# Gated DeltaNet in a hybrid encoder: the transposes of a scan's output stand behind the next head's local part

## The chip, the cores and the metric

The kernel runs on one core of one Trainium2 chip. The metric is the device time of one execution in microseconds (us); lower is better. The core's engines are TensorE (PE; its weight loads are listed apart as PEld), VectorE (DVE), ScalarE (ACT), GpSimd (POOL) and SyncE (SP), which issues the DMAs here. Each engine works through its own instructions in the order in which they stand in the program, and semaphores make one wait for another.

## The reference

An encoder of two layers over 512 tokens of width 1024, all in float32. Layer 0 mixes the tokens with a gated DeltaNet of 8 heads of width 128, layer 1 with HGRN2. Behind each mixer comes a squared-ReLU MLP (1024 to 4096 and back), and at the end an RMSNorm.

```python
for i in range(DEPTH):                      # DEPTH = 2
    y = _rmsnorm(h, norm_mix[i])
    if i % N_MIXERS == 0:
        y = _gated_deltanet(y, gdn_w_in[j], gdn_conv[j], ..., gdn_onorm[j], gdn_w_out[j])
    else:
        y = _hgrn2(y, hgrn_w_in[j], lower_bounds[i], hgrn_gnorm[j], hgrn_w_out[j])
    h = h + y
    h = h + _sq_relu_mlp(_rmsnorm(h, norm_mlp[i]), mlp_w_up[i], mlp_w_down[i])
return _rmsnorm(h, norm_final)
```

The gated DeltaNet projects the input to q, k, v and a gate, runs a short causal convolution and SiLU over q, k and v, normalises q and k, and then works through the tokens of each head in chunks. Per chunk a triangular system is solved, and a state S (128 x 128) is carried from chunk to chunk:

```python
def step(S, xs):
    qd, a_c, u_c, w_c, kd, dl = xs
    v_new = u_c - einsum('bhck,bhkv->bhcv', w_c, S)
    o = einsum('bhck,bhkv->bhcv', qd, S) + einsum('bhij,bhjv->bhiv', a_c, v_new)
    S = S * dl[..., None, None] + einsum('bhck,bhcv->bhkv', kd, v_new)
    return S, o
```

The output o of each head is normalised to unit mean square, scaled by a learned vector, multiplied with the gate and projected by `gdn_w_out`.

## The kernel before

**Numbers and tiles.** Every large product is made of three matmuls of reduced float32 (fp32r): both factors are split into a high and a low part, and lines 125 to 127 add high x high, high x low and low x high. One such matmul takes a 128 x 128 block of the weights and all 512 tokens (128x512 in the profile). `weights` loads a slice of the weights by a DMA of 1 MB on SP's queue (line 108, two buffers `raw`), ScalarE casts the high part (line 114), VectorE subtracts for the low part (line 115). A chunk is 128 tokens here, four per head (NC = 4).

**One head of the DeltaNet** goes through these functions:

- `gdn_conv`: the projections `pj` of q, k and v of the head, the convolution on VectorE and ScalarE (lines 389 to 393).
- `gdn_local`: what needs no state. TensorE transposes k (`pk`, line 436); ScalarE squares it with sums over rows (438), VectorE scales it (440). The same for q (`pq`, lines 443 and 445), then for v (`pv`, line 456, scaled by ScalarE in line 458). A matmul `pe` spreads the decay (462, used on VectorE in 465). Then `pga`, the products of k with k and q (475, in two halves), from which VectorE makes the triangular matrix `n` (477) and the attention matrix `aa` (479). The last line 479 is the last VectorE step of this function.
- `gdn_inverse`, for two heads at once: the triangular matrices are inverted from 32 x 32 blocks up. The first stages are many matmuls of 32x32 (`px`, line 513, and `pu`, line 520), copied out on ScalarE (516), with masks and transposes on VectorE (506 to 508, 522, 523); later stages are lines 531 to 558.
- `gdn_scan`: four chunks one after the other. Per chunk `pks` (585) and VectorE's remainder `r` (587), `pw` with the inverse (590) and VectorE's `wv` (592), the update of the state `ps` (595) and VectorE's `s` (598 or 600), the output `po` (602 and 604). Behind the last chunk: ScalarE squares the output with row sums (611), VectorE adds up `xo` (612 to 614), the inverse root takes two steps on ScalarE and three on VectorE (`rsqrt`, lines 149 to 153), ScalarE scales the output by it (617, into a buffer that the trace names `wlo`), TensorE transposes the four chunks (`pt`, line 620), VectorE multiplies with the learned vector and writes `oh` (622).
- `gdn_gated`: `oh` times the gate, split for the output projection.

**Order.** `gdn` (lines 271 to 323) interleaves the heads: round j projects head j + 1, runs the scan of an earlier head, the local part of head j, and in every second round the inverse of heads j - 2 and j - 1. The scans of heads 0 to 4 come in rounds 3 to 7, which have a local part; those of heads 5, 6 and 7 come in rounds 8 and 9, which have none.

```python
GATES = ((), (), (), (), (0,), (), (1,), (), (2,), (3,))
SCANS = ((), (), (), (0,), (1,), (2,), (3,), (4,), (5,), (6, 7))
```

A scheduler sets each engine's order from the program order, from the dependences, and from priorities: what stands under `high_priority` comes ahead of projections as soon as its inputs are there by the scheduler's reckoning, and projections fill the rest. `after(i, prev)` adds a dependence of the kind NoSync: it orders instruction i behind prev for the scheduler, and sets no semaphore between engines.

**PSUM.** The products of scan and local part share the tag "ma" with two banks (`mix`); head 7's scan and the inverse use "mb" with three; projections have three banks of their own (`acc`). A new tile takes the bank of the oldest and waits until that one's readers are done.

Of the kernel before, what the change touches and what calls it, by code (L numbers as in the profile page):

```python
# [15 lines left out]
ALU = mybir.AluOpType  # L16
PSUM = bass.MemoryType.PSUM

T, D, HID, NH, P = 512, 1024, 4096, 8, 128
# [3 lines left out]
NC = T // P  # L23
# [7 lines left out]
SCANS = ((), (), (), (0,), (1,), (2,), (3,), (4,), (5,), (6, 7))  # L31


class Net:
# [236 lines left out]
    def gdn(self, first):  # L271
        nc, a = self.nc, self.a
        self.emask = self.const("emask", [P, P])
        self.conv = self.const("conv", [P, 3 * NH, 4])
        self.onorm = self.const("onorm", [P, 1])
        self.pick = self.const("pick", [4 * NH, 2 * NH])
        alog = self.cp.tile([P, NH], F32, tag="alog", name="alog")
        nc.sync.dma_start(out=alog, in_=a["alog"].partition_broadcast(P))
        dtb = self.cp.tile([P, NH], F32, tag="dtb", name="dtb")
        nc.sync.dma_start(out=dtb, in_=a["dtb"].partition_broadcast(P))  # L280

        abraw = self.work("gate", [P, NB, 2 * NH], bufs=2)
        nc.sync.dma_start(out=abraw, in_=a["gdn_ab"])
        ab = self.work("x", [P, NB, 4 * NH], F32R)
        hi = ab[:, :, 0:2 * NH]
        nc.scalar.copy(out=hi, in_=abraw)
        nc.vector.tensor_tensor(out=ab[:, :, 2 * NH:], in0=abraw, in1=hi.bitcast(F32), op=ALU.subtract)


        blocks = self.stream(a["gdn_in"][0:3 * NH // 2], self.y, first, 2, spare=1)  # L290
        blocks = chain([next(blocks) for _ in range(6)], blocks)
        with self.tc.high_priority(offset=3000):
            self.rb = self.rstd_rows()
            self.gdn_decay(ab, alog, dtb)


        self.two = True
        xa, xb = (self.wp.tile([P, 4, T], F32, tag=t, bufs=1, name=self.name(t)) for t in ("whi3", "wlo3"))
        self.extra = dict(kq=xa[:, 0:2], v=xa[:, 2], kd=xa[:, 3], aa=xb[:, 0], n=xb[:, 1], ot=xb[:, 2], w2=xb[:, 3])
        self.o, self.on = [None] * NH, [None] * NH  # L300
        hd = {0: self.gdn_conv(0, blocks)}
        self.gdn_silu([hd[0]])
        for j in range(NH + 2):
            todo = []
            if j + 1 < NH:
                hd[j + 1] = self.gdn_conv(j + 1, blocks)
                todo.append(hd[j + 1])
            sg = []
            for i in GATES[j]:
                sg += self.gdn_gates(i)  # L310
            with self.tc.high_priority(offset=3000):
                for i in SCANS[j]:
                    self.gdn_scan(i, hd)
                if j < NH:
                    self.gdn_local(j, hd)
                if 2 <= j <= NH and j % 2 == 0:
                    self.gdn_inverse((j - 2, j - 1), hd)
                if todo or sg:
                    self.gdn_silu(todo, sg)
            for h, t in sg:  # L320
                self.gdn_gated(h, t)
        self.nw_tiles, self.two = 0, False
        self.h = [self.load_x(c) for c in range(NB)]
# [96 lines left out]
    def col(self, n, c, h):  # L420
        return self.cols[n][:, c, h:h + 1]

    def gdn_local(self, h, hd):

        nc, mm, ident = self.nc, self.nc.tensor.matmul, self.ident
        kq, v = hd[h]
        k, q = kq[:, 0], kq[:, 1]
        ck = lambda t, c: t[:, c * P:(c + 1) * P]
        col = lambda n, c: self.col(n, c, h)


        ssk, ssq = self.work("ssk", [P, NC]), self.work("ssq", [P, NC], bufs=5)
        kd, e = self.slot("kd", h, 4), self.work("e")
        pk = self.mix("pk")
        for c in range(NC):
            nc.tensor.transpose(ck(pk, c), ck(k, c), ident)
        for c in range(NC):
            nc.scalar.activation(out=ck(kd, c), in_=ck(pk, c), func=AF.Square, accum_out=ssk[:, c:c + 1])
        for c in range(NC):
            nc.vector.tensor_scalar(out=ck(kd, c), in0=ck(pk, c), scalar1=col("ekl", c), scalar2=None, op0=ALU.mult)  # L440
        pq = self.mix("pq")
        for c in range(NC):
            nc.tensor.transpose(ck(pq, c), ck(q, c), ident)
        for c in range(NC):
            nc.scalar.activation(out=ck(e, c), in_=ck(pq, c), func=AF.Square, accum_out=ssq[:, c:c + 1])
        xk, irk, nd = (self.work(n, [P, NC]) for n in ("xk", "irk", "nd"))
        dd = self.work("dd", [P, NC], bufs=5)
        nc.vector.tensor_scalar(out=xk, in0=ssk, scalar1=EPS, scalar2=None, op0=ALU.add)
        rk = self.rsqrt(xk, "rk")
        nc.vector.tensor_tensor(out=irk, in0=xk, in1=rk, op=ALU.mult)  # L450
        nc.vector.reciprocal(out=dd, in_=xk)
        nc.vector.tensor_tensor(out=dd, in0=dd, in1=self.cols["beta"][:, :, h], op=ALU.mult)
        nc.vector.tensor_scalar(out=nd, in0=dd, scalar1=-1.0, scalar2=None, op0=ALU.mult)
        pv = self.mix("pv")
        for c in range(NC):
            nc.tensor.transpose(ck(pv, c), ck(v, c), ident)
        for c in range(NC):
            nc.scalar.activation(out=ck(v, c), in_=ck(pv, c), func=AF.Copy, scale=irk[:, c:c + 1])


        pe = self.mix("pe")
        mm(pe, lhsT=self.both[:, h:h + 1].to_broadcast([P, P]), rhs=self.rows, start=True, stop=True)
        eg = self.work("x")
        for c in range(NC):
            nc.vector.scalar_tensor_tensor(out=ck(e, c), in0=ck(pe, c), scalar=col("gc", c), in1=self.emask,
                                           op0=ALU.subtract, op1=ALU.add)
        self.act(eg, pe, AF.Exp)
        self.act(e, e, AF.Exp)


        n, aa = self.slot("n", h, 3), self.slot("aa", h, 4)
        for c2 in range(0, NC, 2):
            pga = self.mix("pga", [P, 2, 2, P])
            for c in (c2, c2 + 1):
                mm(pga[:, c - c2], lhsT=ck(k, c), rhs=kq[:, :, c * P:(c + 1) * P], start=True, stop=True)  # L475
            for c in (c2, c2 + 1):
                nc.vector.scalar_tensor_tensor(out=ck(n, c), in0=pga[:, c - c2, 0], scalar=nd[:, c:c + 1],
                                               in1=ck(e, c), op0=ALU.mult, op1=ALU.mult)
            nc.vector.tensor_tensor(out=aa[:, c2 * P:(c2 + 2) * P].rearrange("p (c t) -> p c t", c=2),
                                    in0=pga[:, :, 1],  # L480
                                    in1=e[:, c2 * P:(c2 + 2) * P].rearrange("p (c t) -> p c t", c=2), op=ALU.mult)

        nc.gpsimd.tensor_tensor(out=q, in0=eg, in1=q, op=ALU.mult)
        hd[h] = (kq, kd, v, q, aa, n, ssq, dd)

    def gdn_inverse(self, heads, hd):

# [74 lines left out]
    def gdn_scan(self, h, hd):  # L562

        nc, mm, ident = self.nc, self.nc.tensor.matmul, self.ident
        kq, kd, vr, qd, aa, n, ssq, dd, u = hd[h]
        k = kq[:, 0]
        ck = lambda t, c: t[:, c * P:(c + 1) * P]
# [3 lines left out]
        tag = "mb" if last else "ma"  # L571
# [8 lines left out]
        for c in range(NC):  # L580
            if s is None:
                r = ck(vr, c)
            else:
# [4 lines left out]
                                               op0=ALU.mult, op1=ALU.add)  # L588
# [4 lines left out]
            if c < NC - 1:  # L593
# [5 lines left out]
                else:  # L599
                    nc.vector.scalar_tensor_tensor(out=sn, in0=s, scalar=col("egl", c), in1=ps,  # L600
                                                   op0=ALU.mult, op1=ALU.add)
# [6 lines left out]
        ot = self.extra["n" if last else "ot"]  # L608
# [6 lines left out]
        ro = self.rsqrt(xo, "ro")  # L615
        for c in range(NC):
            nc.scalar.activation(out=ck(ot, c), in_=ck(po, c), func=AF.Copy, scale=ro[:, c:c + 1])
        pt = self.mix("pt", tag=tag)
        for c in range(NC):
            nc.tensor.transpose(ck(pt, c), ck(ot, c), ident)  # L620
        self.on[h] = self.work("oh", bufs=NH)
        nc.vector.tensor_scalar(out=self.on[h], in0=pt, scalar1=self.onorm, scalar2=None, op0=ALU.mult)


    def hgrn(self):
# [411 lines left out]
```

## Time and profile before

| | us |
|---|---|
| three runs | 1355.7, 1358.24, 1358.74 |
| median | 1358.24 |
| the profiled execution, its own time | 1358.3 |
| its span, first to last instruction | 1356.4 |
| TensorE busy | 1330.5 |
| VectorE busy | 820.1 |
| ScalarE busy | 547.0 |
| GpSimd busy | 170.8 |

The profiled execution was recorded by the hardware; its span leaves out 1.9 us around the program. The mean clock that TensorE was granted is 0.994 of full speed. A row of a timeline begins with the start in us and the listed duration, then engine, line, operation, output<-inputs, tile, and how many equal instructions it groups; a bracket names the idle time ahead of it and what ended it. A row of waits has the sum in us, how often, and the longest. "issue" is time for which the profile shows nothing that was waited for. Matmuls overlap, so the distance between two starts says more of TensorE's pace than the listed durations do.

### The profile page before, as it was taken

What the parts mean: (1) busy time and instruction counts of PE and PEld (TensorE: products, weight loads), DVE (VectorE), ACT (ScalarE), POOL (GpSimd) and SP (SyncE); (2) the same over time, 40 slices, a digit from 0 to 9 for tenths busy, and PEclk for the clock granted to TensorE, in tenths of its full rate; (3) what the DMA queues carried; (4) which work ended last, traced back from release to release, by engine and by line L of the source; (5) the groups of instructions that cost most, each with busy time, mean ns of one, the idle gap of its engine ahead of it and who ended that gap; (6) DMA issues with size and microseconds to landing.
All of it is one profiled execution on the core that took longest, in us unless ns stands there. A gap on an engine that the chain in (4) does not pass through costs nothing.

```text
span 1356.4 us, 24202 instructions
## 1 busy us (share of the span) xinstructions
PE 1330.5 (98%) x10340; PEld 1102.9 (81%) x10340; DVE 820.1 (60%) x1408; ACT 547.0 (40%) x1016; POOL 170.8 (13%) x172
## 2 busy tenths in 40 slices
PE   7999999999999999999999999999999999999997
PEld 5777777877888888888888898898888888888897
DVE  5896877765944444444473897787674444445453
ACT  5663556454344214233123555545344313214242
POOL 4001020200200120201220010000100020110222
PEclk8999999999999999999999999999999999999999
DMA  6131111221332222222231311121142223232242
GB/s 200 40 118 35 62 64 34 79 79 64 124 113 100 94 97 93 94 93 94 93 97 42 111 65 64 64 94 64 63 155 93 93 96 113 93 104 93 93 141 78
DMA packets 23356, 121.57 MB, mean 90 GB/s; under 512 B 3664, under 2 KB 6864, under 8 KB 9680
## 3 DMA queue, kind: packets, MB, share of 16 engines
q1 hardware_dynamic: 23248, 120.02, 26.3%
q8 instruction: 81, 1.33, 0.4%
q14 instruction: 27, 0.22, 0.0%
HBM read 117.91 MB, written 2.10 MB: 88 GB/s over the span
## 4 chain that ended last, share of the span: by engine, by line
PE 89%; DVE 5%; ACT 2%; issue 1%; DMA 1%; POOL 0%; SPq 0%; POOLq 0%; DVEq 0%; ACTq 0%
PE pj L126 25%; PE pj L127 25%; PE pj L125 25%; PE pj L714 1%; PE pj L715 1%; PE pj L713 1%; PE pga L475 1%; PE gr L786 1%; PE pu L520 1%; PE px L513 1%; DVE whi L742 1%; DVE wlo L115 1%; PE pw L590 1%; DVE kq L393 1%; DVE ol L742 1%
## 5 line engine op out<-in xcount | busy, mean ns | idle before, releaser
L114 ACT CAST whi<-raw 128x1024 fp32r<-128x1024 f32 (+2 forms) x222 | 220.9, 1024 | 410.0 <-PE pj L126 396.6
L125 PE MATMUL pj<-yh,whi 128*128 128x512 f32 x960 | 381.0, 397 | 0.9 <-ACT whi L114 0.9
L126 PE MATMUL pj<-yl,whi 128*128 128x512 f32 x960 | 381.3, 397 | 0.0
L115 DVE TENSOR_TENSOR wlo<-raw,whi 128x1024 fp32r<-128x1024 f32 (+2 forms) x217 | 289.7, 1348 | 151.0 <-ACT whi L114 148.7
L127 PE MATMUL pj<-yh,wlo 128*128 128x512 f32 x960 | 380.0, 396 | 0.0
L125 PEld LDWEIGHTS pj<-yh,whi 128*128 128x128 f32 x960 | 181.7, 189 | 37.6 <-ACT whi L114 2.0
L126 PEld LDWEIGHTS pj<-yl,whi 128*128 128x128 f32 x960 | 181.9, 189 | 36.0
L127 PEld LDWEIGHTS pj<-yh,wlo 128*128 128x128 f32 x960 | 181.2, 189 | 36.2 <-POOL wlo L115 0.3
L126 PE MATMUL pj<-ol,whi 128*128 128x512 f32 x336 | 131.3, 391 | 0.0
L898 DVE TENSOR_TENSOR gate<-pj,rB 128x512 f32<-128x512 f32 x56 | 38.6, 691 | 148.2 <-PE pj L127 148.2
L125 PE MATMUL pj<-oh,whi 128*128 128x512 f32 x320 | 125.1, 391 | 0.0
L127 PE MATMUL pj<-oh,wlo 128*128 128x512 f32 x320 | 125.0, 391 | 0.0
L884 ACT ACTIVATE z<-pj 128x512 f32<-128x512 f32 x64 | 38.0, 594 | 113.7 <-PE pj L127 109.6
L900 POOL TENSOR_TENSOR kd<-kd,gate 128x512 f32<-128x512 f32 x18 | 23.3, 1293 | 462.2 <-DVE gate L898 462.2
L126 PEld LDWEIGHTS pj<-ol,whi 128*128 128x128 f32 x336 | 63.2, 188 | 13.0
L125 PEld LDWEIGHTS pj<-oh,whi 128*128 128x128 f32 x320 | 60.1, 188 | 12.5 <-issue 0.3
L127 PEld LDWEIGHTS pj<-oh,wlo 128*128 128x128 f32 x320 | 60.0, 188 | 12.2
L165 POOL TENSOR_TENSOR sqacc<-sqacc,z 128x512 f32<-128x512 f32 x25 | 38.0, 1519 | 245.9 <-ACT z L163 241.8
L127 PE MATMUL pj<-kq,wlo 128*128 128x512 f32 (+1 forms) x192 | 67.8, 355 | 0.5 <-DVE wlo L115 0.5
L125 PE MATMUL pj<-kq,whi 128*128 128x512 f32 (+1 forms) x192 | 68.0, 354 | 0.0
L126 PE MATMUL pj<-kq,whi 128*128 128x512 f32 (+1 forms) x192 | 67.9, 354 | 0.0
L742 DVE TENSOR_TENSOR whi<-whi 128x256 f32<-128x256 f32 x112 | 49.9, 447 | 6.4 <-ACT whi L745 4.8
(379 smaller groups left out, 1941.0 us busy)
## 6 DMA issues: line engine op xcount, KB each, us to landing
raw<-down SPq DMA_DIRECT2D x36, 1024.0 KB, 4.9
raw<-up SPq DMA_DIRECT2D x32, 1024.0 KB, 4.8
raw<-gdn_in SPq DMA_DIRECT2D x14, 1024.0 KB, 4.8
raw<-hgrn_fq SPq DMA_DIRECT2D x8, 1024.0 KB, 4.9
raw<-gdn_out SPq DMA_DIRECT2D x4, 1024.0 KB, 5.4
raw<-hgrn_i SPq DMA_DIRECT2D x4, 1024.0 KB, 5.0
raw<-hgrn_gate SPq DMA_DIRECT2D x4, 1024.0 KB, 4.8
raw<-hgrn_out SPq DMA_DIRECT2D x4, 1024.0 KB, 4.9
```

The costliest lines, as they stand in the source:

```text
L114: self.nc.scalar.copy(out=hi[:, k], in_=raw[:, k])
L115: eng.tensor_tensor(out=lo[:, k], in0=raw[:, k], in1=hi[:, k].bitcast(F32), op=ALU.subtract)
L125: mm(o, lhsT=hi[:, k, c], rhs=yh, start=(k == 0), stop=False)
L126: mm(o, lhsT=hi[:, k, c], rhs=yl, start=False, stop=False)
L127: mm(o, lhsT=lo[:, k, c], rhs=yh, start=False, stop=(k == NB - 1))
L165: e.tensor_tensor(out=self.sq, in0=self.sq, in1=t, op=ALU.add)
L393: nc.vector.scalar_tensor_tensor(out=dst[:, s:], in0=z[:, :T - s], scalar=w[:, 3 - s:4 - s], in1=dst[:, s:], op0=ALU.mult, op1=ALU.add)
L475: mm(pga[:, c - c2], lhsT=ck(k, c), rhs=kq[:, :, c * P:(c + 1) * P], start=True, stop=True)
L742: mul = lambda o, x, y: nc.vector.tensor_tensor(out=o, in0=x, in1=y, op=ALU.mult)
L884: nc.scalar.activation(out=z, in_=out, func=AF.Relu)
L898: nc.vector.tensor_tensor(out=t, in0=out, in1=self.r2b, op=ALU.mult)
L900: e.tensor_tensor(out=self.h[c], in0=self.h[c], in1=t, op=ALU.add)
```

## The change

`gdn_scan` no longer issues the transposes `pt` and the VectorE step `oh`; it returns a function `turn` that does. `gdn` calls the scans of the round, then the local part, which now returns its last VectorE step, and then each `turn`. Where there is a local part, each transpose is ordered behind that step by `after`.

```diff
@@ gdn
-                for i in SCANS[j]:
-                    self.gdn_scan(i, hd)
-                if j < NH:
-                    self.gdn_local(j, hd)
+                turn = [self.gdn_scan(i, hd) for i in SCANS[j]]
+                later = self.gdn_local(j, hd) if j < NH else None
+                for t in turn:
+                    t(later)
@@ gdn_local
-            nc.vector.tensor_tensor(out=aa[:, c2 * P:(c2 + 2) * P].rearrange("p (c t) -> p c t", c=2),
+            end = nc.vector.tensor_tensor(out=aa[:, c2 * P:(c2 + 2) * P].rearrange("p (c t) -> p c t", c=2),
...
         hd[h] = (kq, kd, v, q, aa, n, ssq, dd)
+        return end
@@ gdn_scan
-        pt = self.mix("pt", tag=tag)
-        for c in range(NC):
-            nc.tensor.transpose(ck(pt, c), ck(ot, c), ident)
-        self.on[h] = self.work("oh", bufs=NH)
-        nc.vector.tensor_scalar(out=self.on[h], in0=pt, scalar1=self.onorm, scalar2=None, op0=ALU.mult)
+
+        def turn(later):
+            pt = self.mix("pt", tag=tag)
+            for c in range(NC):
+                m = nc.tensor.transpose(ck(pt, c), ck(ot, c), ident)
+                if later is not None:
+                    self.after(m, later)
+            self.on[h] = self.work("oh", bufs=NH)
+            nc.vector.tensor_scalar(out=self.on[h], in0=pt, scalar1=self.onorm, scalar2=None, op0=ALU.mult)
+        return turn
```

The number of instructions on each engine is the same. In the changed kernel the lines behind the first edit shift: the transposes are line 623 and `oh` line 627 there, and lines 506 to 617 of before are one higher.

**TensorE behind head 0's scan.** Before, the transposes of head 0's output stand between projections, some 30 rows behind the scan's last output matmul, and the local part of head 3 begins behind them:

```order
L127 MATMUL pj_1417<-yh_179,wlo_1411 128x512
L620 MATMUL pt_1516<-ident,wlo_68_465 128x128 x2
L125 MATMUL pj_1604<-yh_93,whi_1410 128x512
L620 MATMUL pt_1516<-ident,wlo_68_465 128x128 x2
L436 MATMUL pk_1526<-ident,kq_781 128x128 x4
L126 MATMUL pj_1604<-yl_94,whi_1410 128x512
L127 MATMUL pj_1604<-yh_93,wlo_1411 128x512
L443 MATMUL pq_1539<-ident,kq_781 128x128 x4
```

Now the k transposes of head 3 stand right behind the last output matmul. Between them and the q transposes are 16 projections, then two more up to the v transposes:

```order
L605 MATMUL po_1447<-s_1481,kq_466 128x128
L436 MATMUL pk_1519<-ident,kq_781 128x128 x4
L126 MATMUL pj_1378<-yl_171,whi_1340 128x512
...
L126 MATMUL pj_1417<-yl_132,whi_1410 128x512
L443 MATMUL pq_1532<-ident,kq_781 128x128 x4
L127 MATMUL pj_1417<-yh_131,wlo_1411 128x512
L125 MATMUL pj_1417<-yh_146,whi_1410 128x512
L456 MATMUL pv_1558<-ident,v_782 128x128 x4
```

The transposes of head 0 stand behind the second half of `pga`, directly ahead of head 1's scan:

```order
L475 MATMUL pga_1583<-kq_781 128x256 x2
L125 MATMUL pj_1604<-yh_122,whi_1410 128x512
L126 MATMUL pj_1604<-yl_123,whi_1410 128x512
L127 MATMUL pj_1604<-yh_122,wlo_1411 128x512
L125 MATMUL pj_1604<-yh_131,whi_1410 128x512
L126 MATMUL pj_1604<-yl_132,whi_1410 128x512
L623 MATMUL pt_1590<-ident,wlo_68_465 128x128 x4
L591 MATMUL pw_1767<-v_491,uw_959 128x128
L127 MATMUL pj_1604<-yh_131,wlo_1411 128x512
```

So the local part moved ahead by some 30 rows, and the transposes behind it.

**TensorE in the scan of head 5**, beside the inverse of heads 6 and 7. Before, the 32x32 blocks of `px` are cut once here, by the scan:

```order
L590 MATMUL pw_3509<-r_3507,uw_2892 128x128
L126 MATMUL pj_3968<-yl_108,whi_3961 128x512
L513 MATMUL px_3587<-wd_3574,n_2877 32x32 x16
L513 MATMUL px_3587<-wd_3574,n_3419 32x32 x9
L595 MATMUL ps_3513<-wv_3511,kd_2498 128x128
L602 MATMUL po_3495<-wv_3511,aa_2557 128x128
L604 MATMUL po_3495<-s_3502,kq_1601 128x128
L513 MATMUL px_3587<-wd_3574,n_3419 32x32 x7
L127 MATMUL pj_3968<-yh_107,wlo_3962 128x512
```

Now the scan and the blocks stand closer together, and the next block `pu` is cut twice:

```order
L514 MATMUL px_3587<-wd_3574,n_2870 32x32 x16
L514 MATMUL px_3587<-wd_3574,n_3412 32x32 x5
L591 MATMUL pw_3509<-r_3507,uw_2892 128x128
L514 MATMUL px_3587<-wd_3574,n_3412 32x32 x11
L127 MATMUL pj_3468<-yh_170,wlo_3435 128x512
L596 MATMUL ps_3513<-wv_3511,kd_2491 128x128
L603 MATMUL po_3495<-wv_3511,aa_2550 128x128
L605 MATMUL po_3495<-s_3502,kq_1601 128x128
L521 MATMUL pu_3622<-ud_3573,xd_3620 32x32 x2
L586 MATMUL pks_3519<-s_3515,kq_1601 128x128
L521 MATMUL pu_3622<-ud_3573,xd_3620 32x32 x17
L591 MATMUL pw_3523<-r_3521,uw_2892 128x128
```

What moved here is where the wide matmuls fall into the small ones; their number is the same.

**SP's queue** in the same stretch: the weight loads of the output projection (`raw`, from `gdn_out`) and the loads of x for the residual (line 267, into buffers that scans free). Before:

```order
L108 DMA raw_4203<-gdn_out 128x2048
L108 DMA raw_4342<-gdn_out 128x2048
L267 DMA kd_4185<-x 128x512
L267 DMA aa_4187<-x 128x512
L267 DMA n_4183<-x 128x512
```

Now:

```order
L108 DMA raw_4203<-gdn_out 128x2048
L267 DMA kd_4185<-x 128x512
L267 DMA aa_4187<-x 128x512
L108 DMA raw_4342<-gdn_out 128x2048
L267 DMA n_4183<-x 128x512
```

The third weight load moved behind two loads of x.

## The prediction

> **What bounds the kernel now.** I read the page first: engine shares and chain of waits. Then the waits of the stretch that the change touches, then the timeline around single transposes.
>
> ```profile
> PE 1330.5 (98%) x10340; PEld 1102.9 (81%) x10340; DVE 820.1 (60%) x1408; ACT 547.0 (40%) x1016; POOL 170.8 (13%) x172
> ...
> PE 89%; DVE 5%; ACT 2%; issue 1%; DMA 1%; POOL 0%; SPq 0%; POOLq 0%; DVEq 0%; ACTq 0%
> ```
>
> TensorE is busy for 98% of the span and carries 89% of the chain. So the time is the sum of what TensorE executes, plus what it idles or loses between instructions. Work on the other engines costs nothing unless TensorE stands for it.
>
> By the order of instructions in the program, the two versions agree on TensorE up to the end of head 0's scan and again from some 340 us on; everything the change can do directly lies in about 129 to 340 us. Only heads 0 to 4 have a next local part behind which their transposes can go; for heads 5, 6 and 7 the transposes stay behind their scan.
>
> ```profile
> 128.97:310.00 181.03, 178.12 (x2530) 139.51 (x2528) 131.70 (x341) 97.98 (x283) 22.70 (x39) 1.00 0.18 60
> 292.00:311.00 19.00, 17.54 (x512) 12.98 (x511) 8.02 (x22) 9.20 (x25) 2.96 (x10) 1.00 0.18 64
> 340.00:350.00 10.00, 10.00 (x46) 8.28 (x45) 7.58 (x17) 5.82 (x8) 3.41 (x3) 1.00 0.32 105
> ```
>
> These rows give stretch, length, and then the busy time of TensorE first. From 129 to 310 us TensorE is idle for 181.03 - 178.12 = 2.9 us only, and half of that, 19.00 - 17.54 = 1.5 us, lies in 292 to 311. The last row is pure projection: 46 matmuls of 128x512 in 10 us, so one each 10 / 46 = 0.22 us (0.23 where I take it from start times). A larger distance between two starts is a loss that need not show as idle time, since a listed duration is longer than the pitch.
>
> **The waits that the change can remove.** First the loads of weights into TensorE (PEld), then TensorE itself, with the sum in us, the times and the longest.
>
> ```profile
> PEld pt L620 <- ACT wlo L617: 1.8, 4, 0.8
> PEld pq L443 <- DVE oh L622: 0.9, 4, 0.4
> ```
> ```profile
> 228.61 0.51 PE L127 MATMUL pj<-yh,wlo 128*128 128x512 f32 x1
> 229.57 0.33 PE L620 MATMUL pt<-ident,wlo 128*128 128x128 f32 x1 [0.45 <-ACT wlo L617]
> ```
> ```profile
> PE pu L520 <- issue: 1.3, 2, 1.1
> PE pt L620 <- ACT wlo L617: 0.6, 2, 0.5
> ```
>
> The first fence is the stretch 128 to 290 us, which holds the transposes of heads 0 to 4: their loads wait 1.8 us for ScalarE's scaling of the output (line 617), and the next head's q transposes (line 443) wait 0.9 us for the VectorE step that empties the transposes' PSUM bank. Together 2.7 us, the ceiling of what the move can save. The floor is the idle time of TensorE itself for the same cause, 0.6 us. The pair in the middle tells which end is nearer: the transpose starts 229.57 - 228.61 = 0.96 us behind a projection, 0.96 - 0.23 = 0.73 us late, of which the idle time shows only 0.45 and the load's wait 0.8. So about 0.73 / 0.8 = 0.9 of a load's wait is lost: 0.9 x 1.8 = 1.6 us. The q waits cost less:
>
> ```profile
> 135.35 0.39 PE L127 MATMUL pj<-yh,wlo 128*128 128x512 f32 x1
> 135.65 0.58 PE L620 MATMUL pt<-ident,wlo 128*128 128x128 f32 x2
> 135.99 0.48 PE L125 MATMUL pj<-yh,whi 128*128 128x512 f32 x1
> 136.31 0.45 PE L620 MATMUL pt<-ident,wlo 128*128 128x128 f32 x2
> 136.59 0.60 PE L436 MATMUL pk<-ident,kq 128*128 128x128 f32 x4
> 136.95 0.48 PE L126 MATMUL pj<-yl,whi 128*128 128x512 f32 x1
> 137.26 0.40 PE L127 MATMUL pj<-yh,wlo 128*128 128x512 f32 x1
> 137.60 0.66 PE L443 MATMUL pq<-ident,kq 128*128 128x128 f32 x4
> 138.01 0.47 PE L125 MATMUL pj<-yh,whi 128*128 128x512 f32 x1
> ```
>
> In head 0 the q transposes start 0.34 us behind a projection, 0.11 late. I count 0.4 of the 0.9 us. **Term 1: -2.0 us, bounds -2.7 and -0.6.**
>
> **What is late next.** With the transposes gone from their place, the k transposes of the next head stand right behind the scan's last output matmul, and they take the free one of the two PSUM banks; the q transposes wait for the k bank's readers, and the v transposes (line 456) take the bank that holds the scan's output. That bank is free when line 617 is done: the same releaser as before, with another waiter. In head 0:
>
> ```profile
> 128.75 0.39 PE L604 MATMUL po<-s,kq 128*128 128x128 f32 x2
> ```
> ```profile
> 129.17 0.28 ACT L611 ACTIVATE wlo<-po 128x128 f32<-128x128 f32 x1 [5.79 <-PE po L604]
> ...
> 135.23 1.14 ACT L617 ACTIVATE wlo<-po,ror 128x128 f32<-128x128 f32 x4 [2.21 <-DVE ror L153]
> ```
> ```profile
> 131.29 1.23 DVE L115 TENSOR_TENSOR wlo<-raw,whi 128x1024 fp32r<-128x1024 f32 x1
> ...
> 133.17 1.22 DVE L115 TENSOR_TENSOR wlo<-raw,whi 128x1024 fp32r<-128x1024 f32 x1
> ```
>
> The output matmuls end at 129.14 and line 617 ends at 136.37, 7.2 us later, because VectorE does two weight subtractions between the small steps of the inverse root. In the changed order these two stand behind the root, with shorter steps in between: 7.2 - 2.45 leaves 4.8 us. Between the last output matmul and the v transposes TensorE now has 18 projections and two groups of four transposes: 18 x 0.23 + 0.36 + 0.41 = 4.9 us (136.59 to 136.95 and 137.60 to 138.01 are the pitches of such groups), and a few tenths for going from transposes to wide matmuls. So the v transposes come about when the bank is freed: a miss of up to some 0.5 us in head 0, less in the others, where more stands between. If the cover is gone in all five, the waits come back in full, +1.8. The transposes themselves now wait for the next local part's last step by order alone, with no semaphore between the engines, and line 617 is long done there.
>
> Further, the VectorE step that empties the transposes (0.75 us) now comes ahead of the next scan's first delta step (line 592), which its matmuls wait for; in the new order five projections, 1.1 us, stand between. That covers the 0.75 but little more; a miss of 0.2 in each of five heads is +1.0. **Term 2: +0.8 us, bounds 0 and +2.8.** A wait cannot cost less than nothing. I take a value nearer to the low end, since the cover in head 0 is about as long as the chain and in the other heads longer.
>
> **The small matmuls of the inverse.** Shifting four transposes per head moves where the 32x32 blocks of the inverse (lines 513 and 520) are cut by wide matmuls. In the order of before there are 60 places in this layer where TensorE goes from 32x32 to a wider matmul, in the changed order 66. The cost of one:
>
> ```profile
> 168.47 0.45 PE L513 MATMUL px<-wd,wlo 32*32 32x32 f32 x32
> 168.74 0.48 PE L513 MATMUL px<-wd,n 32*32 32x32 f32 x32
> 169.15 0.50 PE L127 MATMUL pj<-yh,wlo 128*128 128x512 f32 x1
> 169.49 0.39 PE L125 MATMUL pj<-yh,whi 128*128 128x512 f32 x1
> 169.71 0.40 PE L126 MATMUL pj<-yl,whi 128*128 128x512 f32 x1
> ```
>
> The matmul behind the block takes 169.49 - 169.15 = 0.34 us to the next start, where 0.22 follows: 0.11 lost, and about as much ahead of it, where 32 of the block take 0.27 (168.47 to 168.74) but the last 32 take 0.41 to the next start. So 0.22 to 0.25; I take 0.22 x 6. **Term 3: +1.3 us, bounds +0.7 (the later half alone) and +1.3.**
>
> **The instruction stream.** In dense regions of small matmuls TensorE stands with nothing to wait for but its own instructions:
>
> ```profile
> 100.96 0.55 PE L520 MATMUL pu<-ud,xd 32*32 32x32 f32 x41
> 103.62 0.39 PE L520 MATMUL pu<-ud,xd 32*32 32x32 f32 x23 [2.10 <-issue]
> ```
> ```profile
> 305.09 0.43 PE L520 MATMUL pu<-ud,xd 32*32 32x32 f32 x27
> 306.58 0.52 PE L520 MATMUL pu<-ud,xd 32*32 32x32 f32 x37 [1.05 <-issue]
> ```
> ```profile
> 104.40:107.80 3.40, 3.40 (x39) 2.35 (x37) 1.10 (x3) 1.06 (x1) 2.82 (x9) 0.50 0.02 5
> ```
> ```profile
> q8 instruction: 81, 1.33, 0.4%
> ```
>
> The last row counts 81 fetches, 1.33 MB, 16 KB each, over the span. Both stalls stand in the middle of a run of equal matmuls, where, by the count of instructions, a block ends. The third row shows what a long one brings: behind the stall of 2.10 us (2.3 by starts: 103.62 - 100.96, less 0.36 for 41 matmuls) the granted clock is 0.50 for 3.4 us, which costs 3.40 / 2 = 1.7 us more. Small matmuls use up instructions fastest, so that a block has the least time to arrive, and the page lists fetches and weight loads as shares of the same 16 DMA engines. Here the change moves a load, on the queue of SP:
>
> ```profile
> 289.35 0.33 SPq L108 DMA_DIRECT2D raw<-gdn_out  x1
> 291.74 0.33 SPq L267 DMA_DIRECT2D kd<-x  x1
> 294.73 0.33 SPq L267 DMA_DIRECT2D aa<-x  x1
> ```
> ```profile
> raw<-gdn_out SPq DMA_DIRECT2D x4, 1024.0 KB, 5.4
> ```
>
> The third load of the output projection's weights (289.35, 1 MB, 5.4 us to landing) now stands behind the two loads of x, and the second of these is issued only when head 5's scan frees its buffer, at 294.73. So it will occupy the DMA engines from about 295 to 300, in the middle of the 19 us where the inverse of heads 6 and 7 takes instructions fastest. Its own consumer, the third group of the output projection, stands beyond 340 us, so nothing waits for the data; what may wait is TensorE, for its instructions. If that delays by some 0.4 us each the two blocks that TensorE stands for there already (1.3 us, 2 times, above), the term is +0.8. The low end is that all idle time there goes, -1.5; the high end is one more stall like that at 101 us with its half clock, 2.3 + 1.7 = +4.0. The value lies nearer to the stall of 1.05 that this stretch shows than to the 2.10 of the other. **Term 4: +0.8 us, bounds -1.5 and +4.0.**
>
> The Trainium skill, "Runtime: NRT & Kernel Launch", section "Instruction fetch mechanics", says that instructions come in blocks of 16 KiB (256 instructions) which the sequencer fetches ahead by a DMA queue of its own, and that the crossing of a boundary is mostly hidden. By that rule term 4 would be nothing and the sum 0.8 lower. The trace agrees on the size and disagrees on "hidden" in two places, 2.10 and 1.05 us.
>
> **The sum.** The profiled execution took 1358.3 us (span 1356.4 and 1.9 around it); the median of the three runs shown is 1358.24, the same. 1358.3 - 2.0 + 0.8 + 1.3 + 0.8 = **1359.2 us**.
>
> **Rivals.** (A) The forecast: small waits traded for small waits and cuts, the time within 0.2%. A difference of 0.2%, 2.7 us, is about what a measurement of this kernel can tell from no change, so faster means below 1355.6 and slower above 1361.0. For it: no term exceeds 2 us. Chance 0.64. It includes the case that the change does not do what it says: the order between the engines binds the scheduler, not the chip, and were the transposes as late as before, the time would be 1358.3. Against that, the order in the program shows them moved in heads 0 to 4.
>
> (B) Faster: every wait at the transposes goes (-2.7), nothing takes its place, a cut costs its later half (+0.7), and the blocks in 292 to 311 fall so that no fetch is waited for (-1.5): 1358.3 - 3.5 = 1354.8. For it: a boundary shifted by a few instructions can come to lie in a projection, which takes 0.23 us for an instruction or two. Against it: the same dense matmuls are there, and a load was moved beside them. Chance 0.12.
>
> (C) Slower, by one mechanism: the moved weight load holds up one block of instructions in 295 to 305 us until TensorE stands for 2.3 us, and the half clock follows. The place is the inverse of heads 6 and 7, the price 2.3 + 1.7 = 4.0 instead of term 4's 0.8: 1359.2 - 0.8 + 4.0 = 1362.4. It decides from about 2 us of standing at once: 2.10 brought the half clock, 1.05 at 306 did not. For it: the load takes 5.4 us and the stretch already stalls without it. Against: 16 KB is little, and of 81 fetches only three show idle time of TensorE at line 520 (3.4 us in the whole run). Chance 0.24.
>
> The Trainium skill, "TensorE: Matmul & The Clock Gate", section "Why this matters for your kernels", puts the clock's fall behind idle gaps of over some 3 us. By that rule a stall of 2.3 us would leave the clock alone and (C) would give 1.7 less, 1360.7. The trace speaks against it: 0.50 behind 2.10 us.
>
> **How the numbers follow.** The likeliest case is A, 1359.2. The low end is case B, 1354.8; the high end is case C with 0.6 us more for term 2, 1363.0. All high bounds at once (-0.6 + 2.8 + 1.3 + 4.0) would be 1365.8, which I leave out. Faster 0.12, same 0.64, slower 0.24.
>
> **What would show it.** Term 1: in the changed trace no transposes' load waits for the scaling in 128 to 290 us, and the q transposes do not wait for the VectorE step; wrong if over 1 us of either is left. Term 2: the v transposes' loads wait for the scaling, 0.8 us in sum; wrong above 2. Term 3: TensorE's pitch around the blocks as before, six cuts more. Term 4: idle time of TensorE for issue in 292 to 311, about 2 us; rival C if one is above 2 and the clock in the next 3 us is 0.5. The whole is wrong if the time beyond 345 us or ahead of 129 us differs, since nothing stands in another order there: then placement of the blocks, not the transposes, would set the result.

## The result, and the profile after

The changed kernel took 1362.44 us (median of 6 runs, 1361.59 to 1363.04), the kernel before on the same occasion 1357.67 us (6 runs, 1355.7 to 1359.67): a ratio of 1.004, with a 95% interval of 1.003 to 1.005. That is 4.8 us, slower by more than the 0.2% that a measurement of this kernel can tell. The forecast was 1359.2 and "no change"; rival (C), with a chance of 0.24, had named 1362.4.

The profiled executions are 1358.3 us before (0.6 above its median) and 1361.59 after (0.9 below), so the two traces have 3.3 us to explain. First the page of after: the engines' shares and the chain of waits.

```profile
PE 1331.7 (98%) x10340; PEld 1102.8 (81%) x10340; DVE 818.7 (60%) x1408; ACT 545.6 (40%) x1016; POOL 166.4 (12%) x172
...
PE 88%; DVE 6%; ACT 3%; issue 1%; DMA 1%; POOL 0%; SPq 0%; POOLq 0%; DVEq 0%; ACTq 0%
```

Nothing there tells the two kernels apart. The waits of TensorE do, in 290 to 345 us, and then the timeline of TensorE:

```profile
PE pu L521 <- issue: 2.5, 1, 2.5
```
```profile
298.04 0.48 PE L127 MATMUL pj<-yh,wlo 128*128 128x512 f32 x1
298.45 0.60 PE L521 MATMUL pu<-ud,xd 32*32 32x32 f32 x47
301.53 0.34 PE L521 MATMUL pu<-ud,xd 32*32 32x32 f32 x17 [2.48 <-issue]
301.80 0.60 PE L125 MATMUL pj<-yh,whi 128*128 128x512 f32 x1
302.19 0.63 PE L126 MATMUL pj<-yl,whi 128*128 128x512 f32 x1
302.62 0.63 PE L127 MATMUL pj<-yh,wlo 128*128 128x512 f32 x1
```

TensorE stands for 2.5 us in the middle of 64 equal matmuls, with nothing to wait for but its own instructions. The projections behind it start 0.39 to 0.43 us apart where 0.23 was the pitch. The table of stretches (length, then the busy time of TensorE first, and the granted clock behind the five engines) shows why:

```profile
298.80:301.70 2.90, 0.42 (x45) 0.31 (x31) 0.87 (x2) 2.31 (x3) 0.00 (x0) 1.00 0.10 40
...
302.30:305.90 3.60, 3.60 (x70) 2.49 (x70) 2.18 (x5) 0.62 (x1) 0.00 (x0) 0.56 0.02 5
```

The clock is 0.56 for 3.6 us, which costs 0.44 x 3.6 = 1.6 us. In before the longest stand there was 1.05 us, and the clock stayed at 1. What the DMA engines moved in the meantime is told by their rows, each of 40 equal slices; first 293 to 299.2 us, then 299.2 to 301:

```profile
DMA  6139988400000000004930002989897989898971
...
q1 hardware_dynamic: 282, 1.31, 62.9%
...
raw<-gdn_out SPq DMA_DIRECT2D x1, 1024.0 KB, 4.7
```
```profile
q8 instruction: 1, 0.02, 3.4%
```

Up to 299.2 us there is no instruction packet: a load of x, then the 1 MB of weights, which comes in a short burst at about 295.9 us and fills the engines from about 296.7 on. The one packet of instructions comes in the slice behind it, and TensorE goes on 2.3 us later. SP's queue and the engines that free the weight buffer tell why the load lies there. In after:

```profile
289.18 0.33 SPq L267 DMA_DIRECT2D kd<-x  x1
292.07 0.33 SPq L267 DMA_DIRECT2D aa<-x  x1
294.97 0.33 SPq L108 DMA_DIRECT2D raw<-gdn_out  x1
```
```profile
289.87 1.99 ACT L114 CAST whi<-raw 128x1024 fp32r<-128x1024 f32 x2 [3.94 <-PE pj L126]
```
```profile
293.67 1.22 DVE L115 TENSOR_TENSOR wlo<-raw,whi 128x1024 fp32r<-128x1024 f32 x1
```

And the same cast in before:

```profile
283.39 2.00 ACT L114 CAST whi<-raw 128x1024 fp32r<-128x1024 f32 x2 [2.55 <-PE pj L126]
```

The buffer of the third load is that of the first, which ScalarE casts and VectorE subtracts. The cast waits for the projections that still read the old high part. In the changed order scan and inverse stand ahead of those projections, so the cast comes 6.5 us later, the subtraction ends at 294.89, and the load goes out at 294.97 instead of 289.35.

### The profile page after: what moved, and what is told of

The parts are those of the page before. It is cut to its first block, busy times and chain, and to the rows that moved or that the text cites. A ratio compares the mean times of both kernels' runs of the same rounds, so it can differ in the third digit from the quotient of the medians.

```text
span 1359.8 us, 24210 instructions
## 1 busy us (share of the span) xinstructions
PE 1331.7 (98%) x10340; PEld 1102.8 (81%) x10340; DVE 818.7 (60%) x1408; ACT 545.6 (40%) x1016; POOL 166.4 (12%) x172
## 4 chain that ended last, share of the span: by engine, by line
PE 88%; DVE 6%; ACT 3%; issue 1%; DMA 1%; POOL 0%; SPq 0%; POOLq 0%; DVEq 0%; ACTq 0%
PE pj L127 25%; PE pj L126 24%; PE pj L125 24%; PE pj L720 1%; PE pj L721 1%; PE pj L719 1%; PE pga L475 1%; PE gr L792 1%; DVE wlo L115 1%; PE pu L521 1%; PE px L514 1%; ACT whi L114 1%; DVE whi L748 1%; PE pw L591 1%; DVE ol L748 1%
```

## Experiments

Two theories were put to the test. TensorE's instructions come in packets of 16 KB; what one packet brings is called a block here, and the place in the program where a block is used up is its end. F: the 5 us are one fetch of TensorE's instructions, held up by this load, and the half clock behind the stand. W: they are waits and cuts that the moved transposes bring themselves. Beside the total time I use one measure from the traces: the stretch from the first output matmul of head 0's scan that uses the state (line 604, 605 in after) to the last transpose of the HGRN layer (line 802, 808 in after). The work in it is the same in every kernel here but for the change. The groups by tile give it, with first and last start ahead of the shape; before, then after:

```profile
L604 PE MATMUL po<-s,kq x36: 275/275/275, 122.4 to 327.2; 128*128 128x128 f32 x36
```
```profile
L802 PE MATMUL pt<-ident,wlo x24: 272/273/282, 765.3 to 922.7; 128*128 128x128 f32 x24
```
```profile
L605 PE MATMUL po<-s,kq x36: 275/275/275, 122.1 to 328.8; 128*128 128x128 f32 x36
```
```profile
L808 PE MATMUL pt<-ident,wlo x24: 272/273/281, 768.2 to 925.6; 128*128 128x128 f32 x24
```

922.7 - 122.4 = 800.3 us before, 925.6 - 122.1 = 803.5 us after: 3.2 of the 3.3 us lie in this stretch. All runs together ("stretch" by the same two rows of each trace):

| run | kernel | median us (range, runs) | stretch us |
|---|---|---|---|
| | before, beside e1 to e4 (beside e5 to e8 1357.31, beside e9 to e12 1357.14) | 1357.29 (1354.5 to 1360.67, 23) | 800.3 |
| e1 | change | 1362.82 (1362.58 to 1363.78, 5) | 804.1 |
| e2 | change, weight load first in SP's order | 1363.67 (1363.07 to 1365.14, 5) | 805.5 |
| e5 | change, weight load near 315 us | 1360.16 (1359.15 to 1361.46, 11) | 801.7 |
| e3 | before, weight load behind x | 1358.95 (1356.41 to 1360.06, 11) | 801.9 |
| e6 / e4 | before / change, 24 long matmuls added | 1354.57 / 1354.8 | 798.2 / 799.3 |
| e8 / e7 | before / change, 36 long matmuls added | 1358.65 / 1360.38 | 798.2 / 799.6 |
| e9 / e10 | before / change, 24 short matmuls added | 1352.92 / 1353.87 | 798.3 / 799.2 |
| e11 / e12 | before / change, 12 short matmuls added | 1363.5 / 1360.77 | 803.1 / 800.9 |

**e1: the change again,** unedited.

> The changed kernel again, beside the others. Theory F (one fetch of TensorE's instructions is held up by the moved weight load, TensorE stands 2.5 us at 299 us, and half clock follows) and rival W (the moved transposes bring waits and cuts of their own) both expect 1362.4 us, with the profile's stall at 299 us again and a granted clock near 0.5 behind it.

1362.82 us, ratio 1.0041 (1.0029 to 1.0053), with 2.5 us of stand at 300.0 us again. The level and the stand repeat.

**e2: the weight load back ahead of the x loads.** Only SP's order differs:

```diff
+                if norm == 1 and c == 4: [self.after(self.xd[k], self.wd[n0 + 2]) for k in (-5, -4)]
```

(`wd` and `xd` are the lists of weight loads and x loads.)

> The changed kernel with one DMA moved: the third weight load of the output projection stands ahead of the two loads of x again, as in the kernel before; every other engine's order is that of the change. F: the fetch no longer waits for the load, the stall of 2.5 us at 299 us is gone and with it the 1.7 us of half clock; a smaller stall of about 1.2 us may show at the next boundary near 303 us. 1359.0 us, within 1357.5 and 1360.0. W: nothing that the transposes do has changed, 1362.4 us.

A miss: 1363.67 us, ratio 1.0048 (1.0036 to 1.006). SP's queue shows why:

```profile
295.52 0.33 SPq L108 DMA_DIRECT2D raw<-gdn_out  x1
295.89 0.43 SPq L267 DMA_DIRECT2D kd<-x  x1
296.37 0.43 SPq L267 DMA_DIRECT2D aa<-x  x1
```
```profile
PE pu L521 <- issue: 3.3, 1, 3.3
```

First in the queue, the load still goes out at 295.5 us, since its buffer comes free only then; it now holds the x loads back too, and the stand grows to 3.3 us. So the place in SP's order is not what put the load there. The late buffer is.

**e3: the kernel before with the load behind the x loads.**

```diff
+                if norm == 1 and c == 4: self.after(self.wd[n0 + 2], self.xd[-4])
```

> The kernel before with that one DMA moved as the change moves it, behind the two loads of x. F in its full form (the load decides together with where the block ends): the load then transfers at about 296 to 299.4 us, the block that ends at 300.5 to 301 us comes some 0.7 to 1.0 us late where it was 0.2 late, the stall of 0.5 us at 295 us goes, no half clock: 1358.0 us, within 1 us of the kernel before. If the load alone is the cause: 1362 us, a stall of over 2 us near 300. W: as the kernel before.

1358.95 us, ratio 1.0008 (0.9998 to 1.0017): no change that can be told, though the median is 1.7 us above the kernel before where F in its full form had at most 1. The load goes out at 295.83 us, and TensorE stands twice in 290 to 345 us (2.5 us in sum, 1.3 at most; 1.3 in sum in before) with the clock at 1 behind it. The load alone, with the block ending where it ends in before, does not make the 5 us.

**e5: the change with the load out of the way.**

```diff
+                if norm == 1 and c == 4: self.after(self.wd[n0 + 2], self.xd[-6])
```

> The changed kernel with the third weight load of the output projection behind the next two loads of x (the n buffers), so that it is issued near 314 us instead of 295; every other engine's order is that of the change. The earlier attempt to put it ahead changed nothing, since its buffer came free only at 295.5 us. F (the fetch is held up by this load): the fetch starts near 296.5 us, its block is usable near 299, the stall of 2.5 us and its half clock go; about 1 us at the next boundary near 303 us. 1359.2 us, within 1357.5 and 1360.2. W (waits and cuts of the moved transposes): 1362.6 us. If the fetch is late for a reason other than the load: 1362.6 us with the stall still there.

1360.16 us, 2.7 us below e1, with every other engine's order that of the change. The load goes out at 315.19 us. The waits in 290 to 345 us, and the DMA packets in 297.9 to 299.2 us:

```profile
PE pu L521 <- issue: 1.7, 2, 1.2
```
```profile
DMA  0000900000000000000000000000000000000000
...
q8 instruction: 1, 0.02, 6.0%
```

This trace lies 1.0 us behind that of after and level with that of e1: the load of x into `kd` goes out at 290.22 us here, at 290.16 in e1 and at 289.18 in after. So e1 is the one to compare with. There the packet comes at 300.26 us, behind the load's end; here it comes at 298.04, 2.2 us earlier, with the DMA engines free around it. The stand of 2.5 us becomes two short ones, and no half clock follows. That the fetch was held up by the load is shown by this. On the time scale of after the packet comes at 297.0 us, near the expected 296.5.

The second of the short stands shows what is left without a load in the way. TensorE goes on at 300.65 us, the next packet comes 2.95 us later, and TensorE goes on again at 306.19, 127 matmuls and 128 weight loads further on, which is one block (255 instructions in the trace). It had stood for 1.2 us by then: a block of these matmuls was used up in 4.4 us and replaced after 5.5.

The time is 1.0 us above the expected 1359.2, inside its range, and 2.9 above before. Of this the stretch holds 801.7 - 800.3 = 1.4; in the two traces 0.8 us more lies ahead of it and 1.1 behind it, where nothing stands in another order on TensorE, and why is open.

**e4, e6, e7, e8: the block ends moved.** Matmuls are added behind the two warm-up matmuls; each counts four of TensorE's instructions (24 of them add 48 matmuls and 48 weight loads to the trace), so each later block of 256 ends 96 or 144 instructions earlier in the program. The order of the work itself is unchanged on every engine.

```diff
-        for _ in range(2):
-            nc.tensor.matmul(warm, lhsT=zeros[:, 0:P], rhs=zeros[:, 0:WARM], start=True, stop=True)
+        for i in range(24 + 2):
+            nc.tensor.matmul(warm[:, 0:WARM if i < 2 else 8], lhsT=zeros[:, 0:P], rhs=zeros[:, 0:WARM if i < 2 else 8], start=True, stop=True)
```

> The changed kernel with 24 matmuls of 8 columns more among the warm-up matmuls at the start, where TensorE waits for its first data; their result is overwritten. They make every later block of instructions end 96 instructions (24 times 4) earlier in the program. F: the stalls at 101 us and at 299 us both go, each with its half clock (2.3 + 1.7 and 2.6 + 1.7): about 1354 us, within 1352.5 and 1357. W: 1362.4 us, or up to 1 us more for the added matmuls.

> The kernel before with the same 24 small matmuls at the start as e4, so that its blocks end 96 instructions earlier in the program. F: its stalls of 2.3 us at 101 us with the half clock, of 0.5 at 295 and 1.2 at 305 us move; 101 us goes as in e4 (4.0 us). 1353.5 us, within 1352 and 1356, and the difference to the changed kernel with the same addition (1354.8) is under 2 us, of terms 1 to 3 alone. W: the changed kernel stays 5 us slower: 1350 us or 1357 with nothing gained.

> The changed kernel with 36 small matmuls at the start: blocks end 144 instructions earlier. F: no block falls as at 101 us; 1355 us, within 1352.5 and 1358. W: 1362.6 us.

> The kernel before with 36 small matmuls at the start. F: 1354 us, within 1352 and 1357, within 2 us of the changed kernel with the same addition. W: 5 us below the changed kernel with the same addition.

With 24, before and change are 1354.57 and 1354.8 us, ratios of 0.9975 (0.9966 to 0.9985) and 0.9977 (0.9968 to 0.9986) to the plain kernel before: 0.2 us apart where W wanted 5, and inside what F expected of each. The added matmuls hold up the first projection, which starts at 5.25 us in before, at 14.27 in e6's trace, at 11.17 in e4's and at 19.4 in those of e7 and e8, so the totals hold that delay too. With 36 they are 1358.65 and 1360.38, 1.7 apart as F had it, but both levels missed what I expected (1354 and 1355). The stretch is free of the start: 798.2 and 799.3 with 24, 798.2 and 799.6 with 36. Of the four traces only e8's shows TensorE standing for instructions in it, once for 0.8 us, in a projection of the HGRN layer beyond 800 us.

**e9 to e12: the same with matmuls that cost next to nothing.** The added ones are 8x8:

```diff
+            nw, m = (WARM, P) if i < 2 else (8, 8); nc.tensor.matmul(warm[0:m, 0:nw], lhsT=zeros[:, 0:m], rhs=zeros[:, 0:nw], start=True, stop=True)
```

> The kernel before with 24 matmuls of 8x8 behind the two warm-up matmuls: blocks of instructions end 96 instructions earlier, as in e6, but the added matmuls are shorter, so that the start costs less. F: no stall of 2 us at 101 us, none over 0.5 at 290 to 310; 1353 us, within 1350.5 and 1356. W: no view on the level.

> The changed kernel with the same addition as e9. F: no stall over 0.5 us at 290 to 310 us either, so within 2 us of e9, some 1 us above it (the waits and cuts alone): 1354 us. W (the change's own waits and cuts make the 5 us): 5 us above e9.

> The kernel before with 12 of these matmuls: blocks end 48 instructions earlier than in before. F: the stall near 101 us stays (its block still ends among small matmuls, about 1 us earlier), the others move; 1357 us, within 1353 and 1361. W: as before, 1357.3.

> The changed kernel with the same 12. F: the stall near 101 us stays; the block of 299 us ends about 1 us earlier, and its fetch is asked for 1 us earlier: if that is ahead of the weight load's transfer (which begins near 296 us) there is no stall and the time is within 2 us of e11; if it still comes behind the load, the stall is longer than 2.5 us and the time is 4 to 7 us above e11. W: 5 us above e11 in either case, without regard to where idle time stands.

With 24 of them the first projection starts at 5.60 us, 0.35 later than in before. The kernel before comes to 1352.92 us, ratio 0.9969 (0.9957 to 0.9981), the change to 1353.87, ratio 0.9977 (0.9968 to 0.9986): near the 1353 and 1354 that F expected, both faster than either kernel without the addition, and 0.95 us apart. Their rows for 290 to 310, 124 to 341 and 97 to 104 us, before and then the change:

```profile
290.00:310.00 20.00, 20.00 (x483) 14.85 (x484) 11.23 (x24) 11.79 (x28) 3.10 (x10) 1.00 0.14 44
124.00:341.00 217.00, 215.18 (x2794) 170.47 (x2793) 155.58 (x402) 115.59 (x327) 24.48 (x42) 1.00 0.19 65
97.00:104.00 7.00, 6.81 (x230) 5.06 (x217) 4.49 (x9) 2.11 (x4) 2.04 (x6) 1.00 0.44 152
```
```profile
290.00:310.00 20.00, 19.90 (x447) 14.76 (x434) 10.46 (x25) 8.81 (x21) 3.10 (x10) 1.00 0.28 95
124.00:341.00 217.00, 215.52 (x2791) 170.33 (x2790) 152.19 (x400) 112.42 (x325) 19.52 (x41) 1.00 0.19 65
97.00:104.00 7.00, 6.81 (x219) 4.74 (x219) 5.19 (x11) 1.58 (x4) 2.12 (x4) 1.00 0.46 154
```

In the two places where the plain kernels stand, for 2.1 us at 101 us and for up to 2.5 at 290 to 310, TensorE is now idle for 0.2 us at most, and the clock is 1.

With 12 of them the sign turns: before 1363.5 us, ratio 1.0046 (1.0033 to 1.0059), change 1360.77, ratio 1.0021 (1.0009 to 1.0032). Neither W nor a fixed price of the change allows that. For e12 I had expected a time within 2 us of e11, or 4 to 7 us above it; 2.7 us below is a miss. But the condition for no stand came true: the packet comes at 299.98 us, ahead of the weight load, which goes out at 300.74, and TensorE does not stand for instructions in 290 to 310 us. Their waits in 128 to 345 us, before and change:

```profile
PE pu L520 <- issue: 2.3, 2, 1.6
```
```profile
PE pu L521 <- issue: 1.3, 2, 0.9
```

The stretches differ by 2.2 us. TensorE stands 1.0 us less in e12 here, and e11 alone has a half clock behind the 1.6 us (0.68 over 235.3 to 238.7 us and 0.81 over 238.7 to 242.0, which costs 1.7 us) and 1.1 us of stand in the HGRN layer. Together that is 3.8, and the change's own 1 us goes against it.

The level of e11 was a miss too. At 81 to 128 us both stand longer than the plain kernels, 3.3 and 3.7 us against 2.1, but most of it is the clock; before, then e11:

```profile
81.00:128.00 47.00, 43.79 (x766) 33.42 (x753) 33.94 (x75) 21.83 (x47) 5.84 (x13) 0.96 0.21 69
```
```profile
81.00:128.00 47.00, 43.32 (x699) 32.39 (x689) 30.48 (x68) 21.85 (x47) 5.86 (x13) 0.85 0.18 61
```

A clock lower by 0.11 over 47 us costs 5.2 us. The half clock that comes with the stand of 2.3 us lasts 13.7 us in both traces, from about 103 to 117 us, where those in before and after last 3.4; why is open. Both traces are of the slowest execution of their kernel. The executions of e12 scatter over 6.6 us, with a mean clock of 0.996 in the fastest and 0.990 in the slowest.

## Why the prediction was wrong

**The step that failed is term 4,** and with it the choice of the likeliest case. Term 4 reckoned with two fetches late by 0.4 us each. The runs showed one fetch late by 2.2 us (300.26 us in e1, 298.04 in e5 without the load), a stand of 2.5 us and a half clock of 3.4 us behind it. The list of cases did not fail: rival (C) gave the place (the inverse of heads 6 and 7), the mechanism (the third weight load holds up a block of instructions, TensorE stands over 2 us, half clock follows) and 1362.4 us. That this figure is met so closely is in part luck: its 4.0 is a full stand and half clock added, where before's own stands there went away in exchange, and it starts from an execution 0.6 us above the median. I gave it 0.24, on the argument that 16 KB is little and that few of 81 fetches show. The trace of before held the better argument, in SP's queue and in the DMA packets of 101.2 to 102.2 us:

```profile
96.83 0.33 SPq L108 DMA_DIRECT2D raw<-gdn_in  x1
```
```profile
q8 instruction: 1, 0.02, 6.0%
```

The stand that begins at 101.5 us looks like the same event: a load of 1 MB goes out at 96.83, the packet of instructions comes behind it at 101.4, and TensorE goes on at 103.62, 2.2 us behind the packet. No run moved that load, so this is not shown. I had priced that stand, but not looked at what it waited for.

**Term 4** (+0.8, bounds -1.5 to +4.0) measures as follows. Free of stands, the stretch of before is 798.2 to 798.3 us (e6, e9), that of the change 799.2 to 799.3 (e10, e4). So instructions and clock cost 800.3 - 798.3 = 2.0 us in before and 803.5 - 799.3 = 4.2 in after, or 4.8 in e1: the term is +2.2 to +2.8 by the traces. That it is these two is borne out by what TensorE stands for instructions in the stretch plus half the time at half clock: 1.3 us in before, 2.9 + 1.7 in after, 3.0 in e3 (which is 3.6 longer than its stand-free value) and 3.4 + 1.7 in e11 (4.8 longer). The medians of the kernels, 1357.29 and 1362.82, are 5.5 us apart; less the 1 us of terms 1 to 3 that leaves 4.5, so the traces of single executions give about half of it, the runs of before scatter over 6 us, and the other half is open. The step as put was also wrong in its reason: I read the load's delay off SP's order, and e2 showed that the buffer decided.

**Terms 1 to 3** (-2.0, +0.8, +1.3, in sum +0.1) came out at +0.9 and +1.1 by the two pairs without stands (e9 and e10, e6 and e4), and at +1.4 by e8 and e7, where e8 has the one stand of 0.8. The waits that terms 1 and 2 are about are seen at the weight loads in 120 to 285 us, e9 and then e10:

```profile
PEld pt L620 <- ACT wlo L617: 2.2, 5, 0.8
...
PEld ps L595 <- DVE wv L592: 0.9, 5, 0.2
PEld pq L443 <- DVE oh L622: 0.9, 4, 0.4
```
```profile
PEld pe L462 <- ACT wlo L618: 1.4, 3, 0.7
PEld pks L586 <- DVE s L599: 1.4, 3, 0.5
PEld ps L596 <- DVE wv L593: 1.2, 7, 0.2
...
PEld pv L456 <- ACT wlo L618: 0.5, 1, 0.5
```

Term 1 was right in kind: both waits are gone. Term 2 was right in mechanism and too small: the scaling of the output is waited for again, 1.4 + 0.5 = 1.9 us against the 2.2 that went, but mostly by `pe` (line 462) and in three heads, where I had named `pv` and mainly head 0. And the states of the scan (line 599) are waited for by 1.4 us that e9's rows do not have. I had named the first delta step as what the VectorE step of the transposes delays; it moved by 0.3 us (0.9 to 1.2). I count 1.9 + 1.4 + 0.3 = 3.6 us of new waits against 3.1 removed, by loads, of which a part costs time. Other waits fell, though: all rows of this view come to 18.2 us in e9 and 17.0 in e10, and the idle time of TensorE in 124 to 341 us is 1.8 and 1.5 us (the rows above). So the waits do not account for the +1. A loss that shows neither as idle time nor as a wait is left, which is what term 3 says of its six more cuts, but its share was not measured alone, and the cause of the +1 stays open.

**The low end** and rival (B) did not come up. That the places ahead of 129 us and beyond 345 us stay equal held for the two plain traces within 0.5 us each: 3.2 of 3.3 us lie in the stretch. The clause that placement of the blocks would then set the result was nearer the truth than the forecast: it sets it within the stretch.

**Two rules.** By the rule of the Trainium skill, "Runtime: NRT & Kernel Launch", section "Instruction fetch mechanics", that a boundary is mostly hidden, the sum was 1358.4; the traces disagree in e1 (2.5 us), e2 (3.3) and e11 (2.3), and agree in e9. By the Trainium skill, "TensorE: Matmul & The Clock Gate", section "Why this matters for your kernels", a gap has to be over some 3 us; here the trace disagrees: 2.5 us brought 0.56.

## What to carry to other kernels

When a change only reorders work on the engine that bounds the kernel, count where its instruction blocks end before and after, and which large loads are in flight when the next block is due: a block lasted 5.5 us in the inverse here (300.65 to 306.19 us in e5, with 1.2 us of stand), and a load of 1 MB takes 4.7. Compare two versions at several positions of the block ends (a few short instructions at the start shift them all), since one position told +5 us, another +1, and a third -3. If the stands are what costs, shift the block ends first: 24 matmuls of 8x8 gave the kernel before 0.3%, more than the change could have given at best.

## What the runs showed of the hardware

- A fetch of 16 KB waited for a 1 MB load on another queue: in after and e1 its packet is right behind the load's end (299.2 and 300.3 us); in e5 without the load it came 2.2 us earlier than in e1 (298.0).
- The half clock followed stands of 1.56 (e2, clock 0.52 over 103.5 to 106.9 us), 1.58 (e11, 0.68), 2.1 and 2.5 us, and did not follow stands of 1.2 (e5) and 1.3 us (e3). I had put the point at about 2 us. It lasted 3.4 us in before and after, but 13.7 us at the stand of 2.3 us that ends at 104 us in e11 and e12.
- Behind the start of a late packet TensorE went on after 2.2 us (before, 101.4 to 103.6), 2.3 (after) and 2.6 (e5).
- The order of the DMA queue did not decide when a load started where its buffer came free late (e2: first in order it went out at 295.5 us, as third at 295.0 in after and 295.9 in e1).
